# Weight sums of a Strassen pair made together in two buffers, T4 made with T2, and the first down operands fetched among the up products

## The chip, the cores and the metric

The kernel runs on one core of one Trainium2 chip. The metric is the device time of one execution in microseconds (us), the median of the runs shown. The engines are TensorE (PE in the profile's rows, PEld for its weight loads), VectorE (DVE), ScalarE (ACT), GpSimd (POOL) and SyncE (SP), whose queue issues the DMA transfers. Each engine takes its instructions in the order of its own queue and waits on semaphores for the others.

## What is computed

Two transformer blocks in a row, 1024 tokens of width 1024, in f32. Only the two feed-forward networks matter here. In the reference they are

```python
# first block
h = rmsnorm(x, g_ffn[i])
x = x + jnp.square(jax.nn.relu(h @ w_ffn_up[i])) @ w_ffn_down[i]      # 1024 -> 4096 -> 1024
# second block
h = rms_norm(x, g_ffn[l])
up = depthwise_conv(h @ w_up[l], conv_f_w[l], conv_f_b[l], FFN_CONV // 2)   # 1024 -> 2 x 2816, 3 taps
act = jax.nn.gelu(up[..., :D_FF_2], approximate=True) * up[..., D_FF_2:]
x = x + act @ w_down[l]
```

## The kernel before

Every f32 operand is split into a high part rounded to fp32r (`hi`, a copy by ScalarE) and the rest (`lo`, a subtraction by VectorE); a product is three matmuls, high by high, high by low, low by high (`mm3`, L87 to L91). Weights go from DRAM into one of three raw buffers (`wraw`, 128 x 1024, 512 KB) and from there into one of four pairs of split buffers (`whi`, `wlo`).

The **up products** of both networks are made by `strassen` (L1130) with seven products instead of eight (the form of Strassen and Winograd). The contraction of 1024 is halved, and so are the tokens: the normalised input gives the blocks 11, 21 (tokens 0 to 511) and 12, 22 (tokens 512 to 1023), and from these come T1, T2, T3 and T4. Two blocks of 128 weight columns make a pair `j`: the first block holds a11 and a12, the second a21 and a22. From them GpSimd makes the sums S1 = a21 + a22, S2 = S1 - a11 (L1161, L1162), S3 = a11 - a21, S4 = a12 - S2 (L1166, L1167). All four use one buffer `s` with two halves: S1, S2 lie in it until their split is done, then S3, S4 are written over them (S4 reads S2 in its place).

`prep(j, i)` makes the split weights of step `i`: 0 is the raw first block, 1 the sums S1, S2, 2 the sums S3, S4, 3 the block a22. `consume(j, i)` makes the products of the step and adds the results: step 0 the products with 11 and 21, step 1 with T2 and T1, step 2 with T3 and 22, step 3 with T4. One product is 12 matmuls of 128 x 512 into one of six PSUM buffers `p`; VectorE or ScalarE empties it, and GpSimd adds `r` and the "22" result (L1200, L1201, seen in the rows under L1180). `make` finishes a row of results: in the first network the squared relu (L1328), in the second the convolution (ScalarE L1710, VectorE L1711 and L1712), the gelu and the product of both halves (L1728), after which a DMA stores a row of `hid_d`. There are 16 pairs in the first network and 22 in the second. In the loop (L1265 to L1279) the loads of a step are issued three steps ahead (`loads`), `prep` two steps ahead.

**The start.** The last 512 tokens are normalised and transposed in four units (`t_unit`, L1077: two token groups by two halves of the contraction), which give 22, T1, T2, T3; `tf3` and the two `tf` buffers hold what lies between. Meanwhile the step 0 products of the first `npre` pairs run (3 in the first network, 2 in the second). T4 = 21 - T2 is made after that in four units (`t_last`, L1113), two on VectorE and two on GpSimd, spread over the first steps of the loop.

**The turn.** After all up products, `ffn` (L1281) opens the PSUM tiles of the down products (three of 128 x 1024), loads the first down weights, fetches the first rows of `hid_d` (4 rows of 128 in the first network, 2 in the second) into the buffers `hraw`, splits them (`hh`, `hl`), and reads the residual `x` back from DRAM (`xres`, eight tiles of 512 KB); it lies where the buffers of `strassen` lay.

**The order of the queues** is not the order of the code. A planner walks the instructions with a model of their times and puts on each engine's queue the earliest written instruction that is ready in the model; a later one goes ahead where the earlier are not. A buffer is given out again when its last user is done.

Of the kernel before, what the change touches and what calls it, by code (L numbers as in the profile page):

```python
# [27 lines left out]
class Kern:  # L28
# [1048 lines left out]
    def t_unit(self, hs, t0, k0):  # L1077
# [33 lines left out]
        sub(nc.vector, o["T2"][1], f1, f(o["T2"][0]))  # L1111

    def t_last(self, t0, k0):  # L1113

        nc, B = self.nc, self.B
        t = slice((t0 % 4) * P, (t0 % 4 + 2) * P)
        d = (slice(None), slice(k0, k0 + 2), t)
        t2, t4, b21 = ([x[d] for x in B[n]] for n in ("T2", "T4", "21"))
        f = lambda x: x.bitcast(F32)
        a = self.tf3[:, k0 * 256:k0 * 256 + HALF].rearrange("p (k t) -> p k t", k=2)  # L1120
# [9 lines left out]
    def strassen(self, st, w, pairs, sp, make, npre=3):  # L1130
# [21 lines left out]
        def prep(j, i):  # L1152
            tt = nc.gpsimd.tensor_tensor
            if i == 0:
                split(j, 0, raws[j, 0])
                return
            a11, a12 = (raws[j, 0][:, c:c + HALF] for c in (0, HALF))
            a21, a22 = (raws[j, 1][:, c:c + HALF] for c in (0, HALF))
            if i == 1:
                s = ws["s"] = self.sx.tile([P, WCH], F32, tag="s", name="s", bufs=1)  # L1160
                tt(out=s[:, :HALF], in0=a21, in1=a22, op=ALU.add)  # L1161
                tt(out=s[:, HALF:], in0=s[:, :HALF], in1=a11, op=ALU.subtract)  # L1162
                split(j, 1, s)
            elif i == 2:
                s = ws["s"]
                tt(out=s[:, :HALF], in0=a11, in1=a21, op=ALU.subtract)  # L1166
                tt(out=s[:, HALF:], in0=a12, in1=s[:, HALF:], op=ALU.subtract)  # L1167
                split(j, 2, s)
            else:
                split(j, 3, a22)  # L1170
# [38 lines left out]
        seq = [(j, 0) for j in range(npre)]  # L1209
        seq += [(j, i) for j in range(n) for i in range(4) if i or j >= npre]  # L1210
        items = [s for s in seq if s[1] < 3]

        def loads(q):
            if q < len(items):
                j, i = items[q]
                if i == 0 or i == 1 and j < npre:
                    load(j, 0)
                if i == 1:
                    load(j, 1)

# [4 lines left out]
        for q in range(npre):  # L1225
            loads(q)
            prep(*items[q])
            if q == 0:
                for i in range(6):
                    spill(i)  # L1230
# [10 lines left out]
        self.tf3 = self.gp.tile([P, S], F32, tag="gain1024", name="tf3", bufs=self.gb)  # L1241
        hs = self.norm_rows(src, D, gain, (4, 5))
        self.t_unit(hs, 4, 0)
        consume(*seq[0])
# [3 lines left out]
        B["T4"] = [self.sx.tile([P, 4, HALF], F32R, name="T4" + c) for c in "hl"]  # L1248
        self.t_unit(hs, 4, 2)
        consume(*seq[1])  # L1250
        self.t_unit(hs2, 6, 0)
        loads(npre)
        prep(*items[npre])
        self.t_unit(hs2, 6, 2)
        for q in range(2, npre):
            consume(*seq[q])
        rest = [self.t_last(t0, k0) for t0 in (4, 6) for k0 in (0, 2)]
        for r in (rest[0], rest[1], rest[0], rest[2]):
            next(r)
        loads(npre + 1)  # L1260
        prep(*items[npre + 1])
        loads(npre + 2)
        next(rest[2])
        q = npre
        for j, i in seq[npre:]:  # L1265
            if i < 3:
                loads(q + 3)
                if q + 2 < len(items):
                    prep(*items[q + 2])
                q += 1  # L1270
            if i == 2:
                prep(j, 3)
            consume(j, i)
            if rest and j == 0:
                next(rest[1 if i == 1 else 3])
                if i == 1:
                    next(rest[3])
                else:
                    rest = None  # L1279

    def ffn(self, st, nf, w_up, pairs, make, w_down, last=2, gain=None, npre=3):  # L1281
# [3 lines left out]
        self.xs_d = self.dr.tile([S, D], F32, name="xs_d")  # L1285
        with ExitStack() as su:
            self.pp = self.pool(su, "psU", space=PSUM)
            sp = self.pool(su, "sp")
            self.strassen(su, w_up, pairs, sp, make, npre)
# [3 lines left out]
        hid = {}  # L1293

        def fetch(f):
            raw = self.tmp4.tile([P, S], F32, tag="t4", name="hraw")
            nc.sync.dma_start(out=raw, in_=self.hid_d[f * P:(f + 1) * P, :])
            hid[f] = [dp.tile([P, S], F32R, tag="h" + c, name="h" + c, bufs=5) for c in "hl"]
            self.split(*hid[f], raw)
# [3 lines left out]
        for f in range(n):  # L1303
            fetch(f)
# [507 lines left out]
```

## Time and profile before

| | |
|---|---|
| median of 3 runs | 3478.67 us (3476.00 to 3480.02) |
| profiled execution | 3482.99 us, of which span 3481.3 us |
| granted TensorE clock, mean | 0.984 |
| busy: TensorE, VectorE, ScalarE, GpSimd | 3297.0, 1896.1, 1272.3, 599.4 us |
| up products of the first network | about 1135 to 1462 us of the span |
| up products of the second network | about 2725 to 3216 us |

Times in rows count from the span's start. A row of the timeline has start, duration, engine, line, operation, output <- inputs, and in brackets the idle time of the engine before it and who ended it. `SPq` is SyncE's queue. Matmuls are pipelined: one takes 0.39 us from its first to its last word but the next starts after 0.23 us.

### The profile page before, as it was taken

Reading aid. Unit: us, or ns where it says so; the run is one execution under the profiler, and the core shown is the slowest. Engines: PE = TensorE matmul, PEld = TensorE weight load, DVE = VectorE, ACT = ScalarE, POOL = GpSimd, SP = SyncE. Lnnn points to the kernel's source line nnn. Section 1 sums busy time; section 2 is a strip of 40 time slices with the busy share of each in tenths; the row PEclk is TensorE's granted clock in tenths of the full one; section 3 lists DMA queues with packets and bytes.
Section 4 is the critical chain, followed back from the end, with each engine's and each line's share of the span. In section 5 each row is a group of like instructions: output and inputs, shape, how many; then the busy total and the mean of one; then the engine's idle time right before and its main releaser. Section 6 shows DMA issues by size and latency. Waiting matters only on the chain.

```text
span 3481.3 us, 46328 instructions
## 1 busy us (share of the span) xinstructions
PE 3297.0 (95%) x18534; PEld 2696.5 (77%) x18534; DVE 1896.1 (54%) x2829; ACT 1272.3 (37%) x1776; POOL 599.4 (17%) x700
## 2 busy tenths in 40 slices
PE   8999999999989799999999999999999799999899
PEld 8867777777778588788889877777889676776787
DVE  4445666466554654544443466666242866666544
ACT  4342434477422322211122567743121433333211
POOL 0201111122100534200002411100000433333000
PEclk9999999999999899999999999999999999999999
DMA  3532232332372333432221222223353122222521
GB/s 118 169 107 71 74 76 63 92 85 70 123 266 91 106 112 107 167 129 93 90 74 39 96 64 67 66 77 114 123 195 116 65 85 71 71 71 90 184 91 63
DMA packets 362374, 350.89 MB, mean 101 GB/s; under 512 B 88766, under 2 KB 286766, under 8 KB 362158
## 3 DMA queue, kind: packets, MB, share of 16 engines
q1 hardware_dynamic: 362158, 347.93, 31.5%
q8 instruction: 145, 2.38, 0.3%
q14 instruction: 71, 0.58, 0.1%
HBM read 249.29 MB, written 98.58 MB: 100 GB/s over the span
## 4 chain that ended last, share of the span: by engine, by line
PE 61%; DVE 14%; POOL 8%; ACT 6%; issue 6%; DMA 5%; SPq 0%; POOLq 0%; DVEq 0%; ACTq 0%
PE mm L89 16%; PE mm L90 16%; PE mm L91 16%; DVE wlo L59 3%; DMA wraw<-in_w_up_dram 2%; DMA wraw<-in_w_ffn_up_dram 1%; POOL s L1166 1%; POOL s L1167 1%; POOL r L1180 1%; PE p L89 1%; POOL s L1161 1%; PE rps L803 1%; PE p L90 1%; PE p L91 1%; DVE cv L1711 1%
## 5 line engine op out<-in xcount | busy, mean ns | idle before, releaser
L58 ACT CAST whi<-wraw 128x1024 fp32r<-128x1024 f32 (+3 forms) x234 | 232.3, 1001 | 796.9 <-PE mm L91 456.3
L59 DVE TENSOR_TENSOR wlo<-wraw,whi 128x1024 fp32r<-128x1024 f32 (+3 forms) x234 | 279.7, 1203 | 260.7 <-ACT whi L58 255.7
L89 PE MATMUL mm<-whi,hh 128*128 128x512 f32 x864 | 338.1, 393 | 17.2 <-ACT hh L58 12.1
L90 PE MATMUL mm<-wlo,hh 128*128 128x512 f32 x864 | 338.0, 391 | 0.0
L91 PE MATMUL mm<-whi,hl 128*128 128x512 f32 x864 | 336.6, 391 | 0.4 <-DVE hl L59 0.4
L1052 DVE TENSOR_TENSOR xres<-mm,xres 128x512 f32<-128x512 f32 (+1 forms) x272 | 166.4, 653 | 306.4 <-PE mm L91 305.1
L194 POOL TENSOR_SCALAR nst<-nst 128x2 f32<-128x2 f32 (+1 forms) x41 | 9.6, 235 | 1267.5 <-ACT hn L211 1009.2
L89 PEld LDWEIGHTS mm<-whi,hh 128*128 128x128 f32 x864 | 162.8, 189 | 55.4 <-ACT hh L58 12.5
L58 ACT CAST whi<-s 128x1024 fp32r<-128x1024 f32 x76 | 79.9, 1051 | 313.9 <-POOL s L1167 249.8
L91 PEld LDWEIGHTS mm<-whi,hl 128*128 128x128 f32 x864 | 162.8, 189 | 35.6 <-DVE hl L59 1.6
L90 PEld LDWEIGHTS mm<-wlo,hh 128*128 128x128 f32 x864 | 163.3, 189 | 33.8
L89 PE MATMUL mm<-h0h,whi 128*128 128x512 f32 x432 | 167.9, 392 | 3.8 <-ACT h0h L58 1.4
L91 PE MATMUL mm<-h0h,wlo 128*128 128x512 f32 x432 | 169.1, 391 | 0.0
L90 PE MATMUL mm<-h0l,whi 128*128 128x512 f32 x432 | 168.8, 391 | 0.1
L59 DVE TENSOR_TENSOR wlo<-s,whi 128x1024 fp32r<-128x1024 f32 x76 | 97.0, 1276 | 104.9 <-ACT whi L58 104.9
L91 PE MATMUL mm<-h1h,wlo 128*128 128x512 f32 x336 | 131.0, 390 | 0.0
L90 PE MATMUL mm<-h1l,whi 128*128 128x512 f32 x336 | 131.0, 390 | 0.0
L89 PE MATMUL mm<-h1h,whi 128*128 128x512 f32 x336 | 130.7, 390 | 0.0
L89 PE MATMUL p<-h1h,whi 128*128 128x512 f32 x304 | 121.0, 398 | 6.0 <-DVE u L1180 6.0
L89 PE MATMUL p<-h0h,whi 128*128 128x512 f32 x304 | 119.1, 392 | 1.5 <-DVE xres L1052 1.5
L90 PE MATMUL p<-h1l,whi 128*128 128x512 f32 x304 | 119.3, 392 | 0.0
L91 PE MATMUL p<-h0h,wlo 128*128 128x512 f32 x304 | 119.0, 392 | 0.0
(546 smaller groups left out, 8815.4 us busy)
## 6 DMA issues: line engine op xcount, KB each, us to landing
wraw<-in_w_in_dram SPq DMA_DIRECT2D x66, 512.0 KB
hraw<-hid_d SPq DMA_DIRECT2D x54, 512.0 KB
wraw<-in_w_up_dram SPq DMA_DIRECT2D x46, 512.0 KB
wraw<-in_w_ffn_up_dram SPq DMA_DIRECT2D x35, 512.0 KB
hid_d<-o SPq DMA_DIRECT2D x64, 256.0 KB
wraw<-in_w_ffn_down_dram SPq DMA_DIRECT2D x32, 512.0 KB
g<-gate_d SPq DMA_DIRECT2D x24, 512.0 KB
hid_d<-cv SPq DMA_DIRECT2D x22, 512.0 KB
```

Source lines behind the costliest of these rows:

```text
L58: return (self.nc.scalar.copy(out=hi, in_=src), self.nc.vector.tensor_tensor(out=lo, in0=src, in1=hi.bitcast(F32), op=ALU.subtract))
L59: self.nc.vector.tensor_tensor(out=lo, in0=src, in1=hi.bitcast(F32), op=ALU.subtract))
L89: mm(ps, lhsT=sh, rhs=mh, start=first, stop=False)
L90: mm(ps, lhsT=sh, rhs=ml, start=False, stop=False)
L91: mm(ps, lhsT=sl, rhs=mh, start=False, stop=last)
L803: mm(q4(ps)[:, i], lhsT=lhs[:, 4 * h + i], rhs=rhs[:, i], start=True, stop=True)
L1052: self.nc.vector.tensor_tensor(out=o, in0=ps[:, i], in1=o, op=ALU.add)
L1161: tt(out=s[:, :HALF], in0=a21, in1=a22, op=ALU.add)
L1166: tt(out=s[:, :HALF], in0=a11, in1=a21, op=ALU.subtract)
L1167: tt(out=s[:, HALF:], in0=a12, in1=s[:, HALF:], op=ALU.subtract)
L1180: return lambda out: e.tensor_tensor(out=out, in0=a, in1=b, op=ALU.add)
L1711: stt(out=c[:, 1:], in0=u[:, :S - 1], scalar=one("cw0"), in1=c[:, 1:], op0=ALU.mult, op1=ALU.add)
```

## The change

Four things are done. S1, S2 get a buffer `ss[1]` and S3, S4 another, `ss[2]`, which is `tf3`; the four sums of a pair are written one behind the other, in the pair before. The loop over pairs is written out anew with other places for loads, splits and sums. Three of the four T4 units become part of `t_unit` (they use f1 = T2, which is there), on GpSimd; the first is still made by `t_last`, on VectorE. And the first rows of `hid_d` and the first half of the down weights are fetched by `before_last`, called in the last pair between step 1 and step 2, through the `wraw` buffers and into the place of the operands 11 and 21.

```diff
-    def t_unit(self, hs, t0, k0):
+    def t_unit(self, hs, t0, k0, last=True):
...
         sub(nc.vector, o["T2"][1], f1, f(o["T2"][0]))
+        if last:
+            h, l = (f(x[d]) for x in B["21"])
+            sub(nc.gpsimd, f1, h, f1)
+            nc.gpsimd.tensor_tensor(out=f1, in0=f1, in1=l, op=ALU.add)
+            self.t_split(f1, d)
+
+    def t_split(self, src, d):
+        nc, (h, l) = self.nc, (x[d] for x in self.B["T4"])
+        nc.scalar.copy(out=h, in_=src)
+        nc.gpsimd.tensor_tensor(out=l, in0=src, in1=h.bitcast(F32), op=ALU.subtract)
 
     def t_last(self, t0, k0):
...
-        tt = (nc.gpsimd if k0 else nc.vector).tensor_tensor
-        tt(out=a, in0=f(b21[0]), in1=f(t2[0]), op=ALU.subtract)
-        tt(out=a, in0=a, in1=f(t2[1]), op=ALU.subtract)
-        tt(out=a, in0=a, in1=f(b21[1]), op=ALU.add)
-        yield
-        nc.scalar.copy(out=t4[0], in_=a)
-        tt(out=t4[1], in0=a, in1=f(t4[0]), op=ALU.subtract)
-        yield
+        a = self.tmp4.tile([P, S], F32, tag="t4", name="t4f")[:, :HALF].rearrange("p (k t) -> p k t", k=2)
+        tt = self.nc.vector.tensor_tensor
+        f = lambda n, c: self.B[n][c][d].bitcast(F32)
+        tt(out=a, in0=f("21", 0), in1=f("T2", 0), op=ALU.subtract)
+        tt(out=a, in0=a, in1=f("T2", 1), op=ALU.subtract)
+        tt(out=a, in0=a, in1=f("21", 1), op=ALU.add)
+        self.t_split(a, d)
...
         def prep(j, i):
+            split(j, i, raws[j, 0] if i == 0 else raws[j, 1][:, HALF:] if i == 3 else ss[i])
+
+        def sums(j, i):
...
+            s1, s2, s3, s4 = (ss[q][:, c:c + HALF] for q in (1, 2) for c in (0, HALF))
             if i == 1:
-                s = ws["s"] = self.sx.tile([P, WCH], F32, tag="s", name="s", bufs=1)
...
+                tt(out=s1, in0=a21, in1=a22, op=ALU.add)
+                tt(out=s2, in0=s1, in1=a11, op=ALU.subtract)
             else:
-                split(j, 3, a22)
+                tt(out=s4, in0=a12, in1=s2, op=ALU.subtract)
+                tt(out=s3, in0=a11, in1=a21, op=ALU.subtract)
...
+        self.tf3 = ss[2] = self.gp.tile([P, S], F32, tag="gain1024", name="tf3", bufs=self.gb)
         hs = self.norm_rows(src, D, gain, (4, 5))
+        self.t_unit(hs, 4, 0, False)
+        consume(0, 0)
         hs2 = self.norm_rows(src, D, gain, (6, 7))
...
+        ss[1] = self.sx.tile([P, WCH], F32, name="s12")
         self.t_unit(hs, 4, 2)
+        sums(0, 1)
+        consume(1, 0)
         self.t_unit(hs2, 6, 0)
+        prep(0, 1)
         self.t_unit(hs2, 6, 2)
+        sums(0, 2)
+        load(1, 0)
+        self.t_last(4, 0)
+        for j in range(2, npre):
+            consume(j, 0)
+        for j in range(n):
+            if j >= npre:
+                consume(j, 0)
+            prep(j, 3)
+            prep(j, 2)
+            if j + 1 < n:
+                load(j + 1, 1)
+            consume(j, 1)
+            if j + 1 < n:
+                if j + 1 >= npre:
+                    prep(j + 1, 0)
+            else:
+                before_last()
+            if j + 2 < n:
+                load(j + 2, 0)
+            consume(j, 2)
+            if j + 1 < n:
+                sums(j + 1, 1)
+                sums(j + 1, 2)
+            consume(j, 3)
+            if j + 1 < n:
+                prep(j + 1, 1)
...
+        def fetch(f, raw, place):
+            nc.sync.dma_start(out=raw, in_=self.hid_d[f * P:(f + 1) * P, :])
+            hid[f] = place
+            self.split(*hid[f], raw)
+
+        def before_last():
+
+            n = nf % 4 or 4
+            place = [t.rearrange("p k t -> p (k t)").rearrange("p (k t) -> p k t", k=4) for t in self.first()]
+            for f in range(n):
+                fetch(f, self.wps[0].tile([P, WCH], F32, tag="wraw", name="hraw", bufs=self.wrb),
+                      [t[:, f] for t in place])
+            pre.extend(self.load_chunks(w_down, 0, n, cols[:1]))
...
-        pre = self.load_chunks(w_down, 0, n, cols)
-        for f in range(n):
-            fetch(f)
+        pre.extend(self.load_chunks(w_down, 0, len(hid), cols[1:]))
```

The later rows of `hid_d` are fetched as before, through `tmp4`.

## Rows read from the trace of the kernel before

**Rows 1.** Busy us of each engine in six stretches; the first line names the columns.
```profile
core 0: us, PE busy (x) PEld busy (x) DVE busy (x) ACT busy (x) POOL busy (x), PEclk, DMA share, GB/s
...
1179.60:1187.30 7.70, 5.61 (x12) 3.97 (x13) 4.44 (x4) 1.68 (x2) 4.54 (x4) 0.50 0.42 138
1188.00:1462.00 274.00, 273.90 (x1209) 226.33 (x1208) 141.56 (x186) 68.05 (x88) 104.17 (x82) 1.00 0.38 122
2745.80:2788.70 42.90, 32.77 (x120) 25.43 (x121) 38.51 (x31) 15.45 (x19) 32.05 (x19) 0.86 0.09 25
2790.00:3216.00 426.00, 396.14 (x1674) 308.52 (x1673) 270.82 (x278) 158.95 (x181) 147.99 (x116) 1.00 0.24 76
3216.60:3228.80 12.20, 0.18 (x1) 0.00 (x0) 10.49 (x11) 4.53 (x4) 2.48 (x2) 0.71 0.81 271
3228.80:3235.30 6.50, 6.09 (x14) 4.34 (x15) 3.58 (x3) 1.04 (x1) 0.00 (x0) 0.50 0.95 322
```

**Rows 2.** Waits of TensorE, 2600 to 3240 us: total us, times, longest.
```profile
PE p L89 <- DVE u L1180: 27.5, 33, 1.7
PE mm L89 <- ACT hh L58: 12.1, 1, 12.1
```

**Rows 3.** Chain of waits through one pair of the second network: start, us, what.
```profile
3153.79 1.23 DVE wlo L59
3155.15 1.29 POOL s L1166
3156.44 1.26 POOL s L1167
3157.72 3.80 DMA wraw<-in_w_up_dram
3161.66 1.28 POOL s L1161
3163.02 1.29 POOL s L1162
3164.31 1.25 POOL r L1180
```

**Rows 4.** Waits of GpSimd and VectorE, 2790 to 3216 us.
```profile
POOL s L1166 <- DVE wlo L59: 190.7, 19, 10.2
POOL s L1161 <- DMA wraw<-in_w_up_dram: 73.6, 19, 4.5
...
DVE u L1180 <- POOL r L1180: 93.0, 20, 5.4
```

**Rows 5.** VectorE's timeline, second network: a convolution's two steps, an add between.
```profile
3145.96 1.27 DVE L1711 SCALAR_TENSOR_TENSOR cv<-u,vcol_conv_f_b,cv 128x1023 f32<-128x1023 f32 x1
3147.15 0.68 DVE L1180 TENSOR_TENSOR u<-p,tf 128x512 f32<-128x512 f32 x1
3147.75 1.27 DVE L1712 SCALAR_TENSOR_TENSOR cv<-u,vcol_cw,cv 128x1023 f32<-128x1023 f32 x1
```

**Rows 6.** Waits of TensorE, 1100 to 1500 us.
```profile
PE p L89 <- ACT T4h L1126: 13.2, 1, 13.2
...
PE mm L89 <- DVE o L1180: 3.5, 1, 3.5
```

**Rows 7.** Timelines of VectorE, TensorE and GpSimd in the first network's start.
```profile
1140.28 0.68 DVE L1097 TENSOR_TENSOR T2l<-tf,T2h 128x512 fp32r<-128x512 f32 x1
...
1149.70 0.67 PE L89 MATMUL p<-T2h,whi 128*128 128x512 f32 x1 [1.19 <-ACT T2h L1110]
...
1156.78 2.14 POOL L1124 TENSOR_TENSOR tf<-tf,h0l 128x512 f32<-128x512 f32 x1
```

**Rows 8.** VectorE's timeline, "12" adds of the second network's last two pairs.
```profile
3205.66 0.69 DVE L1180 TENSOR_TENSOR u<-p,r 128x512 f32<-128x512 f32 x1 [1.47 <-POOL r L1180]
...
3220.73 0.69 DVE L1180 TENSOR_TENSOR u<-p,r 128x512 f32<-128x512 f32 x1 [1.46 <-POOL r L1180]
```

**Rows 9.** VectorE's and GpSimd's timelines, second network, two steps that overlap.
```profile
2774.58 1.86 POOL L1161 TENSOR_TENSOR s<-wraw 128x512 f32<-128x512 f32 x1 [1.49 <-DMA wraw<-in_w_up_dram]
...
2775.23 2.30 DVE L1711 SCALAR_TENSOR_TENSOR cv<-u,vcol_conv_f_b,cv 128x1023 f32<-128x1023 f32 x1
```

**Rows 10.** VectorE's groups by form, 2790 to 3216 us: busy us, mean ns, idle before.
```profile
L1180 DVE TENSOR_TENSOR u<-p,r 128x512 f32<-128x512 f32 x40 | 27.5, 688 | 93.0 <-POOL r L1180 93.0
```

More of the change, by code (lines that the diff above doesn't have):

```diff
@@ L1111, in t_unit, with strassen @@
         sub(nc.vector, o["T2"][1], f1, f(o["T2"][0]))
+        if last:
[7 more added lines that the diff above has]
+        nc.gpsimd.tensor_tensor(out=l, in0=src, in1=h.bitcast(F32), op=ALU.subtract)
     def t_last(self, t0, k0):
[L1115 removed]
         t = slice((t0 % 4) * P, (t0 % 4 + 2) * P)
         d = (slice(None), slice(k0, k0 + 2), t)
[L1118 to L1130 removed]
+        a = self.tmp4.tile([P, S], F32, tag="t4", name="t4f")[:, :HALF].rearrange("p (k t) -> p k t", k=2)
[5 more added lines that the diff above has]
+        self.t_split(a, d)
+    def strassen(self, st, w, pairs, sp, make, npre, before_last):
         nc = self.nc
@@ L1152, in prep @@
         def prep(j, i):
+            split(j, i, raws[j, 0] if i == 0 else raws[j, 1][:, HALF:] if i == 3 else ss[i])
+        def sums(j, i):
             tt = nc.gpsimd.tensor_tensor
-            if i == 0:
-                split(j, 0, raws[j, 0])
-                return
             a11, a12 = (raws[j, 0][:, c:c + HALF] for c in (0, HALF))
             a21, a22 = (raws[j, 1][:, c:c + HALF] for c in (0, HALF))
+            s1, s2, s3, s4 = (ss[q][:, c:c + HALF] for q in (1, 2) for c in (0, HALF))
             if i == 1:
-                s = ws["s"] = self.sx.tile([P, WCH], F32, tag="s", name="s", bufs=1)
[L1161 to L1168, printed above, removed]
-            else:
-                split(j, 3, a22)
+                tt(out=s1, in0=a21, in1=a22, op=ALU.add)
+                tt(out=s2, in0=s1, in1=a11, op=ALU.subtract)
+            else:
+                tt(out=s4, in0=a12, in1=s2, op=ALU.subtract)
+                tt(out=s3, in0=a11, in1=a21, op=ALU.subtract)
+        ss = {}
         def product(j, i, q, b):
@@ L1208, in strassen @@
         n = len(pairs)
[L1209 to L1219, printed above, removed]
         self.sx = None
@@ L1224, in strassen @@
         spill = lambda i: nc.sync.dma_start(out=x_d[i * P:(i + 1) * P, :], in_=x[i])
[L1225 to L1230, printed above, removed]
+        for j in range(npre):
+            load(j, 0)
+            prep(j, 0)
+        for i in range(6):
+            spill(i)
+        load(0, 0)
+        load(0, 1)
         for i in (6, 7):
@@ L1248, in strassen @@
         B["T4"] = [self.sx.tile([P, 4, HALF], F32R, name="T4" + c) for c in "hl"]
+        ss[1] = self.sx.tile([P, WCH], F32, name="s12")
         self.t_unit(hs, 4, 2)
-        consume(*seq[1])
+        sums(0, 1)
+        consume(1, 0)
         self.t_unit(hs2, 6, 0)
-        loads(npre)
-        prep(*items[npre])
+        prep(0, 1)
         self.t_unit(hs2, 6, 2)
[L1255 to L1279, printed above, removed]
+        sums(0, 2)
[25 more added lines that the diff above has]
+                prep(j + 1, 1)
     def ffn(self, st, nf, w_up, pairs, make, w_down, last=2, gain=None, npre=3):
@@ L1285, in ffn @@
         self.xs_d = self.dr.tile([S, D], F32, name="xs_d")
+        hid, pre = {}, []
+        cols = [(0, 512), (512, 512)]
+        def fetch(f, raw, place):
[9 more added lines that the diff above has]
+            pre.extend(self.load_chunks(w_down, 0, n, cols[:1]))
         with ExitStack() as su:
@@ L1288, in ffn @@
             sp = self.pool(su, "sp")
-            self.strassen(su, w_up, pairs, sp, make, npre)
+            self.strassen(su, w_up, pairs, sp, make, npre, before_last)
         self.pp = self.pool(st, "psD", space=PSUM)
@@ L1292, in ffn @@
         dp = self.pool(st, "hid")
[L1293 to L1299, printed above, removed]
-        cols = [(0, 512), (512, 512)]
-        n = nf % 4 or 4
-        pre = self.load_chunks(w_down, 0, n, cols)
-        for f in range(n):
-            fetch(f)
+        pre.extend(self.load_chunks(w_down, 0, len(hid), cols[1:]))
         xp = self.pool(self.xst, "x", side="right")
@@ L1311, in ffn @@
             n = (nf - f0) % 4 or 4
-            for f in range(max(f0 + 1, len(hid)), min(f0 + n + 1, nf)):
-                fetch(f)
+            for f in range(len(hid), min(f0 + n + 1, nf)):
+                fetch(f, self.tmp4.tile([P, S], F32, tag="t4", name="hraw"),
+                      [dp.tile([P, S], F32R, tag="h" + c, name="h" + c, bufs=5) for c in "hl"])
             x = lambda k, hf: [t[:, hf * HALF:(hf + 1) * HALF] for t in hid[f0 + k]]
```

3 lines of the change are left out of this document (removed).

## The prediction

> **What bounds the kernel now.** I first read the busy time by stretches [rows 1], because the change touches only the two feed-forward networks and their ends. In the up products of the first network TensorE is busy for all of 274.0 us with 1209 matmuls, 0.2266 us each; a pair of column blocks is 7 products of 12 matmuls, so 84 x 0.2266 = 19.04 us is the pace that TensorE can hold. In the second network the like stretch has 1674 matmuls (19.93 pairs) in 426.0 us, 21.38 us a pair: 1674 x 0.2266 = 379.4 us, so 46.6 us are lost, though both stretches run at the full granted clock, 2.4 GHz. Around them stand shorter losses: the starts, and the turn from up to down products.
>
> Next the waits of TensorE [rows 2]: in the second network it waits 33 times for VectorE's adds (L1180), which free a product's PSUM buffer, and once 12.1 us for the first down operand. So VectorE is late, although it is busy for only 270.8 of 426 us. The chain of waits says why [rows 3]: the low split of S1, S2 releases GpSimd's S3 (1.29 us), S4 (1.26 us) frees a raw weight buffer, the load of the next pair's second weight block takes 3.80 us, S1 and S2 of the next pair follow, and only behind them does GpSimd reach the add r of this pair, for which VectorE holds the evacuation of the "22" product. The list of waits puts sizes on it [rows 4]: over 19 pairs S3 waits 190.7 us for the split, S1 73.6 us for the load, and the add 93.0 us (20 pairs, 4.65 us each) for r. This loop, not an engine's work, makes 21.4 us a pair. In the first network VectorE has no convolution to do and the same loop fits under 19.04 us.
>
> Queues are not in written order [rows 5]: the "21" add is written behind both steps of a convolution and runs between them. The planner fills a gap with later work that is ready.
>
> In the first network's start TensorE waits 13.2 us for T4 and at the turn 3.5 us for VectorE [rows 6]; T4's last part starts only when GpSimd gets to it (its steps there take up to 2.14 us [rows 7]), and behind the wait TensorE ran at half clock, 1.2 GHz, for 7.7 us [rows 1].
>
> **The change, part by part.** Durations are those of the one profiled execution, 3482.99 us (span 3481.3 us, 1.7 us around it). It stands 4.3 us above the median of 3478.67, so I subtract from 3482.99 and then take 4.3 off.
>
> *Sums in two buffers, up loop (second network).* Compute is the same: four sums, four splits, two loads a pair. What goes is the tie: S3, S4 no longer wait for the split of S1, S2, and all four are written ahead of the pair's last product. Moved past on GpSimd: sums now stand behind r and the "22" sum of the pair before, not ahead of them. On SP the two loads stand a half pair earlier in the written loop; a load waits for S4 of an earlier pair, and behind it in SP's queue wait a pair's stores, which nobody needs for a long time. The splits move too: that of S1, S2 is written behind the whole evacuation of a pair, 24 matmuls (5.4 us) ahead of its use; hidden only if the planner pulls it forward, as it does now [rows 5]. What is late next? Either TensorE (19.04) or VectorE beside GpSimd. VectorE alone: from the "12" add of the last pair but one to that of the last, where no sums stand on GpSimd, it took 3220.73 - 3205.66 = 15.07 us [rows 8]. The sums come back beside its work: a convolution step that meets one took 2.30 instead of 1.27 us [rows 5, 9], 1.03 us more. Four of them: 15.07 + 4 x 1.03 = 19.2 us. Bounds: 19.04 (nothing collides) and 21.0, VectorE and GpSimd strictly one after the other (270.8 + 148.0 us over 19.93 pairs [rows 1]). The 15.07 + 4.1 is the nearest; with 0.2 us for hand-overs I take **19.4**. That gives back 0.36 x 19.93 = 7.2 of 46.6 us: a gain of **39.4** us, ends 46.6 and 7.
>
> The Trainium skill, SBUF — State Buffer, section Who interferes with whom, speaks against putting GpSimd's sums beside VectorE: a VectorE instruction with two SBUF inputs and a GpSimd instruction that reads SBUF shut each other out, and the one issued second waits for the end of the first. The trace agrees (1.27 against 2.30 us). It leaves adds that read PSUM free, five of 0.69 us a pair [rows 10]: 21.0 - 3.4 = 17.6 us of exclusive time, so by the rule alone the period would be TensorE's 19.04 and this term 46.6.
>
> In the first network the loop is already at TensorE's pace; no gain, and no loss as long as VectorE (141.6 of 274 us) keeps its room.
>
> *T4 beside T2, start of the first network.* Before, two of four T4 units were VectorE's and two GpSimd's, 4 steps each; now three are GpSimd's altogether, the fourth only in its last step: GpSimd 10 steps for 8, VectorE 3 for 8, ScalarE 4 as before. The new cost is order: S3, S4 of pair 0 go into the buffer that the units use for T3 (L1095), so they stand behind the last T3 unit and, on GpSimd, behind T4. From the second unit's T2 (1140.28 + 0.68 [rows 7]) GpSimd has 14 steps up to S3, about 1.5 us each (1.29 to 2.14 [rows 3, 7]): 1141 + 21 = 1162; split 1163. TensorE starts T2 at 1149.7 [rows 7], has 36 matmuls (8.2 us) besides T3, waits some 4 us, then does T3, T4 with half of it at half clock: 1171. The next pair's S1 waits for a raw buffer that S4 frees: 1162 + 3.8 + 2.6 + a split of 1 = 1169.5, in time. TensorE got there at 1187.3 before, with about 1 us of the next product done: gain 15, I take **14**. Ends: 24 (60 matmuls from 1149.7 without a wait end at 1163.3) and 4 (GpSimd at 2.14 us a step: split at 1172, then 24 matmuls at half clock, 0.46 us each as in the 6.5 us stretch [rows 1], end at 1183).
>
> *The same start, second network.* 42.9 us for 120 matmuls, which need 27.2 [rows 1]: 15.7 lost. TensorE has one product pair less to hide GpSimd's steps (two blocks are prepared, not three). Lost in my count above: 1171 - 1149.7 - 13.6 = 8; some 3.5 more here: gain **4**, ends 12 and -5.
>
> *First down operands in the last pair.* Two fetches (four in the first network) and one (two) weight loads are issued on SP through the three raw weight buffers, their splits into the buffer of operands 11 and 21, free after the last pair's first two products, 60 matmuls (13.6 us) before the turn. Behind the splits' wait on ScalarE stand copies of the last pair; the planner places a split when its load can have landed. VectorE has room, since no next pair's splits come. In the second network TensorE stood 12.2 us, then 14 matmuls took 6.5 us at half clock for 3.2 [rows 1]: 15.5 in all. What stays is the evacuation of the last product, some 3.5 us as in the first network [rows 6]. The x reload, 4.19 MB at the 322 GB/s seen there, 13 us, is now met sooner; three PSUM tiles of 2.7 us cover 8 of it: 1 us more. Gain **11**, ends 15 and 2. In the first network the turn is 3.5 us, bound by VectorE: gain **1.5**, ends 3.5 and -2. The second half of the down weights is loaded after the turn's start in the written order; it is needed 5.4 us or more later and its buffers free during the last pair: nothing, at worst the 3.8 us of a load.
>
> Sum: 39.4 + 14 + 4 + 11 + 1.5 = 69.9. 3482.99 - 69.9 = 3413.1, less 4.3: **3408.8**, say 3409.
>
> **Rivals.** (a) *VectorE and GpSimd become the bound*: the sums hit more often, six steps instead of four, and in-order queues leave gaps; 20.5 us a pair, near the serial 21.0. For it: 2.30 against 1.27. Against: five adds read PSUM, and TensorE may run six PSUM buffers ahead. The loop then gains 46.6 - 1.46 x 19.93 = 17.5: 3431. The skill's rule above is the reason; taken alone it does not reach 20.5.
>
> (b) *GpSimd's backlog eats the starts*: 2.14 us a step instead of 1.5 puts S3 9 us later; the starts give 2 instead of 18: 3425.
>
> (c) *The loop stays*: the load still lands too late, behind SP's queue, and a pair takes 21.38: only 30.5 of gain: 3448. Against: S4 no longer waits for a split.
>
> (d) *Slower: the written order becomes the queue's.* Then the split of S1, S2 is VectorE's last work of a pair, and TensorE stops at T2 of every pair of the second network: the rest of T2 and T1, 22 matmuls, 5.0 us, then VectorE's chain of 15.07 with four collisions, 4.1: 24.2 us a pair, 2.8 x 19.93 = 56 lost, less the 30.5 won elsewhere: 3504. It decides above 21.38 + 30.5 / 19.93 = 22.9 us a pair. Against it: [rows 5], and operands that today are split well before use.
>
> **Numbers.** Forecast 0.62 (its own range 3388 to 3428), (a) 0.16, (b) 0.10, (c) 0.05, (d) 0.07. The range 3386 to 3446 takes in the forecast, (b), nearly all of (a). No change means within 0.2%, about 7 us, which is what a measurement of this kernel can tell: only the tails between (c) and (d), 0.03. Slower 0.07, faster 0.90.
>
> **What would show it.** Right: 1674 matmuls of the second network's up products in 379 to 390 us; r no longer behind S1, S2; the wait for T4 gone, a smaller one for T3 in its place; no wait for hh at the turn. Wrong: VectorE's two-input steps at 2.3 us throughout (a); TensorE waiting for the low split at T2 in each pair (d); starts that last as long as now (b).

## The result and the profile after

The changed kernel takes **3416.36 us** in the median of 4 runs (3413.16 to 3416.72) beside 3477.34 for the kernel before in the same series: a ratio of 0.9823, 95% interval 0.9806 to 0.9840. The forecast was 3409, range 3386 to 3446. The profiled execution is 3416.02 us (span 3414.3), 67.0 us shorter than the one before.

To see where these went I cut both spans at the same matmuls: a network's first up product, the last T4 matmul of pair 1, the last up product, the first down product. Times in us:

| stage | before | after | gain | forecast |
|---|---|---|---|---|
| up to the first up product (same program) | 1123.9 | 1117.0 | 6.9 | 0 |
| first network, start, through pair 1's T4 | 76.9 | 64.3 | 12.6 | 14 |
| first network, loop | 261.6 | 267.7 | -6.1 | 0 |
| first network, turn | 3.9 | 4.5 | -0.6 | 1.5 |
| second network, start, through pair 1's T4 | 67.7 | 67.2 | 0.5 | 4 |
| second network, loop | 427.8 | 382.3 | 45.5 | 39.4 |
| second network, turn | 12.5 | 5.9 | 6.6 | 11 |
| down products and all between | 1507.0 | 1505.4 | 1.6 | 0 |

The first row is no effect of the change: it is the same program, and the kernels of the experiments took 1114.0 to 1123.6 us there. Without it some 60 us are left, of which the second loop is three quarters.

Busy time by stretches, after (columns as in rows 1): first network's start and loop, then the second's start, loop and turn.

```profile
1117.00:1181.30 64.30, 53.01 (x215) 42.05 (x216) 51.10 (x55) 23.04 (x38) 44.40 (x30) 0.89 0.28 89
1181.30:1449.00 267.70, 263.03 (x1153) 217.10 (x1152) 142.99 (x185) 70.70 (x87) 108.64 (x82) 0.99 0.41 129
...
2708.30:2775.40 67.10, 49.84 (x194) 39.16 (x192) 47.99 (x52) 27.62 (x43) 45.55 (x30) 0.82 0.20 62
2776.00:3157.50 381.50, 380.65 (x1679) 314.59 (x1678) 291.77 (x286) 160.89 (x185) 166.03 (x117) 1.00 0.28 89
3157.70:3163.60 5.90, 0.42 (x3) 0.05 (x1) 5.63 (x6) 2.59 (x4) 2.86 (x2) 0.71 0.64 206
```

The line from 2776 us on answers [rows 1]: where 1674 matmuls took 426.0 us, 1679 take 381.5, and TensorE is busy for 380.65 of them: 0.227 us a matmul, 19.1 us a pair. The loop runs at TensorE's pace.

The waits of TensorE, second network (2700 to 3200 us), which answer [rows 2]:

```profile
PE tr L1087 <- DVE tf L1097: 11.7, 3, 6.2
PE mm L89 <- DVE u L1181: 5.5, 1, 5.5
PE p L89 <- ACT whi L58: 3.1, 1, 3.1
```

Of the 33 waits for VectorE's adds one of 0.7 us is left, and the wait for `hh` is gone; the turn now waits 5.5 us for VectorE's last add. The rest lies in the start. The first network (1100 to 1480 us, [rows 6]):

```profile
PE p L89 <- ACT whi L58: 5.7, 1, 5.7
...
PE p L89 <- DVE o L1181: 2.4, 1, 2.4
PE p L91 <- DVE a22l L59: 2.3, 1, 2.3
```

The 13.2 us for T4 became 5.7 us for the split of pair 0's S3, S4, ahead of T3. The other two lines, at pair 2's T4, are new.

The waits of GpSimd and VectorE in the second loop (2776 to 3157 us), which answer [rows 4]:

```profile
POOL s L1166 <- DVE wlo L59: 179.4, 18, 10.1
...
DVE u L1181 <- POOL r L1181: 85.2, 20, 4.5
```

GpSimd's wait for the load is gone. But its wait for the low split is as long as ever: it has moved from S3 to S1. And VectorE still waits 4.3 us a pair for r. One pair in the timelines of GpSimd and then VectorE (L1166, L1167 are S1, S2; L1169 S4, L1170 S3) shows the way round, to be laid beside [rows 3] and [rows 8]:

```profile
3060.43 1.30 POOL L1166 TENSOR_TENSOR s<-wraw 128x512 f32<-128x512 f32 x1 [10.13 <-DVE wlo L59]
3061.81 2.16 POOL L1167 TENSOR_TENSOR s<-s,wraw 128x512 f32<-128x512 f32 x1
3064.05 1.29 POOL L1169 TENSOR_TENSOR tf<-wraw,s 128x512 f32<-128x512 f32 x1
3065.30 1.30 POOL L1170 TENSOR_TENSOR tf<-wraw 128x512 f32<-128x512 f32 x1
3066.55 1.29 POOL L1181 TENSOR_TENSOR r<-r,tf 128x512 f32<-128x512 f32 x1
```

```profile
3049.08 0.69 DVE L1181 TENSOR_TENSOR u<-p,r 128x512 f32<-128x512 f32 x1 [4.43 <-POOL r L1181]
...
3059.13 1.22 DVE L59 TENSOR_TENSOR wlo<-s,whi 128x1024 fp32r<-128x1024 f32 x1
...
3060.87 1.94 DVE L59 TENSOR_TENSOR wlo<-tf,whi 128x1024 fp32r<-128x1024 f32 x1
3062.74 0.68 DVE L1181 TENSOR_TENSOR tf<-p,r 128x512 f32<-128x512 f32 x1
3067.87 0.69 DVE L1181 TENSOR_TENSOR u<-p,r 128x512 f32<-128x512 f32 x1 [4.46 <-POOL r L1181]
```

The low split of S1, S2 (3059.13) frees their buffer, S1 of the next pair goes into it at once, the four sums follow, **r only behind them**, then VectorE's "12" add (3067.87), and from there its evacuation down to the next low split. So the loop of before is still closed (a chain of waits that comes back to its own first step, one pair later, and so has a period of its own), but shorter, since the load is no longer in it: from one "12" add to the next 18.79 us. Its margin to TensorE's 19.04 is 0.25 us. Before, two "12" adds lay 21.82 us apart:

```profile
3143.76 0.69 DVE L1180 TENSOR_TENSOR u<-p,r 128x512 f32<-128x512 f32 x1 [4.93 <-POOL r L1180]
...
3165.58 0.69 DVE L1180 TENSOR_TENSOR u<-p,r 128x512 f32<-128x512 f32 x1 [4.95 <-POOL r L1180]
```

### The profile page after: what moved, and what is told of

Its sections match the earlier page's. It is cut to its first block, busy times and chain, and to the rows that moved or that the text cites. A ratio compares the mean times of both kernels' runs of the same rounds, so it can differ in the third digit from the quotient of the medians.

```text
span 3414.3 us, 46299 instructions
## 1 busy us (share of the span) xinstructions
PE 3277.0 (96%) x18534; PEld 2701.3 (79%) x18534; DVE 1898.1 (56%) x2819; ACT 1273.8 (37%) x1776; POOL 628.2 (18%) x704
## 4 chain that ended last, share of the span: by engine, by line
PE 76%; DVE 9%; ACT 5%; issue 4%; POOL 3%; DMA 2%; SPq 0%; DVEq 0%; ACTq 0%; POOLq 0%
PE mm L89 16%; PE mm L90 16%; PE mm L91 16%; PE p L91 6%; PE p L89 6%; PE p L90 6%; PE rps L803 1%; PE tr L236 1%; PE lr L89 1%; PE tp L507 1%; PE rps L719 1%; DVE wlo L59 1%; PE lr L90 1%; DVE sq L1529 1%; PE lr L91 1%
## 5 line engine op out<-in xcount | busy, mean ns | idle before, releaser
L59 DVE TENSOR_TENSOR wlo<-wraw,whi 128x1024 fp32r<-128x1024 f32 (+3 forms) x234 | 281.0, 1209 | 266.9 <-ACT whi L58 261.3
L89 PE MATMUL mm<-whi,hh 128*128 128x512 f32 x768 | 298.4, 391 | 1.4 <-ACT whi L58 1.4
L90 PE MATMUL mm<-wlo,hh 128*128 128x512 f32 x768 | 298.9, 389 | 0.0
L91 PE MATMUL mm<-whi,hl 128*128 128x512 f32 x768 | 298.6, 389 | 0.0
L89 PEld LDWEIGHTS mm<-whi,hh 128*128 128x128 f32 x768 | 143.5, 188 | 34.3 <-ACT whi L58 4.8
L91 PEld LDWEIGHTS mm<-whi,hl 128*128 128x128 f32 x768 | 144.1, 188 | 30.2 <-DVE hl L59 0.2
L90 PEld LDWEIGHTS mm<-wlo,hh 128*128 128x128 f32 x768 | 144.2, 188 | 30.0
L1709 ACT ACTIVATE cv<-u,vcol_conv_f_b,vcol_cw 128x1024 f32<-128x1024 f32 x44 | 54.8, 1246 | 207.7 <-DVE u L1181 136.3
L90 PE MATMUL p<-h0l,whi 128*128 128x512 f32 x304 | 119.9, 394 | 0.0
```

What stands on the lines that cost most here:

```text
L59: self.nc.vector.tensor_tensor(out=lo, in0=src, in1=hi.bitcast(F32), op=ALU.subtract))
L89: mm(ps, lhsT=sh, rhs=mh, start=first, stop=False)
L90: mm(ps, lhsT=sh, rhs=ml, start=False, stop=False)
L91: mm(ps, lhsT=sl, rhs=mh, start=False, stop=last)
L1709: nc.scalar.activation(out=c, in_=u, func=AF.Identity, scale=one("cw1"), bias=one("conv_f_b"))
```

## The experiments

My theory after the comparison: the shared buffer made the second loop, and all of it; what is left is a loop of 18.79 us. Rivals: the order, the loads, or collisions between VectorE and GpSimd.

**Two buffers alone.** Into the kernel before, S3, S4 in `tf3`:

```diff
-                s = ws["s"]
+                s2 = ws["s"]
+                s = self.tf3 if j else s2
...
-                tt(out=s[:, HALF:], in0=a12, in1=s[:, HALF:], op=ALU.subtract)
+                tt(out=s[:, HALF:], in0=a12, in1=s2[:, HALF:], op=ALU.subtract)
```

> The kernel before with one edit: S3, S4 of every pair but the first go into tf3 and not over S1, S2; loads, splits, T4 and the turn stay where they were. Theory (the shared buffer made the loop): from the end of pair 1's T4 product to the last product of the second network 382 to 390 us where before has 427.9 and after 382.3; time about 3434 us, nearly all of the loop's gain. Rival 1 (the new places of loads, sums and splits made it): 420 to 428 us, time 3470 to 3477. Rival 2 (both are needed): between, about 405 us and 3455.

3418.76 us, ratio 0.9835 (0.9816 to 0.9854); second loop 387.5. In this kernel pair 1's S3, S4 overwrite part of the working of T4, so T4 comes out wrong and the starts are not to be used. With `j > 1` in place of `j` that does not happen:

> The kernel before with e1's edit from pair 2 on only (pairs 0 and 1 keep the one buffer), so that nothing is overwritten while T4 is worked out. Theory: the second buffer acts in the steady loop, so the loop of the second network is 386-391 us as in e1 (387.5) and the time 3417-3424. Rival: e1 was short because part of T4's work was spoiled early; then the start or the loop is longer by more than 4 us.

3425.47 us, ratio 0.9860 (0.9844 to 0.9875). Its starts are 4.4 and 5.1 us longer than in the kernel just shown (75.5 and 72.0 for 71.1 and 66.9), so the rival holds for them: that time was too short. The loop is shorter than expected. The second loop and turn:

```profile
2791.00:3172.70 381.70, 381.70 (x1682) 315.93 (x1680) 291.91 (x283) 161.82 (x181) 161.04 (x117) 1.00 0.27 86
3172.70:3178.30 5.60, 0.39 (x3) 0.01 (x1) 5.38 (x5) 3.29 (x3) 0.00 (x0) 0.72 0.85 304
```

The profile shows no idle time of TensorE in the loop. Some 50 of the 61 us (3475.76 - 3425.47, the kernel before in the same series) come from the second buffer; the loop written out anew has no part in them. And the turn fell from 12.5 to 5.6 us **without the early fetch**. SyncE's timeline of before (below it VectorE's last split ahead of the fetch) and of this kernel says how:

```profile
3216.96 6.43 SPq L78 DMA_DIRECT2D wraw<-in_w_down_dram  x3
3223.50 0.41 SPq L1297 DMA_DIRECT2D hraw<-hid_d  x1
```

```profile
3221.34 1.66 DVE L59 TENSOR_TENSOR wlo<-wraw,whi 128x1024 fp32r<-128x1024 f32 x1
```

```profile
3167.07 5.81 SPq L78 DMA_DIRECT2D wraw<-in_w_down_dram  x2
3172.99 0.41 SPq L1298 DMA_DIRECT2D hraw<-hid_d  x1
```

The fetch stands in SyncE's queue behind loads of down weights, and those wait for raw buffers that VectorE's low splits free (the last in the kernel before ended at 3223.00, in this one at 3172.49). In the kernel before VectorE was late, and the fetch went out 7.1 us after the last product had started (3216.4); here 0.3 us after it (3172.7).

**The early fetch taken back**, after the change (`before_last` out, the rows fetched behind the loop as before):

```diff
-            else:
-                before_last()
...
```

> The changed kernel without the early fetch: first rows and first down weights are asked for after the up products, through tmp4, as before. Theory (the early fetch gives the second network's turn and nothing in the first): last up product to first down matmul 12 us in the second network (before 12.4, after 5.9), 3.5 to 5 in the first (before 3.9, after 4.6); time 3423 to 3427. Rival (with VectorE no longer late the late fetch is hidden too): 6 us, time 3416 to 3418.

3412.05 us (3411.07 to 3413.18), ratio 0.9817 (0.9802 to 0.9831); turns 2.3 and 5.7 us. The rival holds: in the changed kernel the early fetch brings nothing that can be told. In the first network it costs 2.2 us at the turn, as one more split stands ahead of VectorE's last add; in the second the wait for `hh` is back and VectorE's is gone, of nearly the same length (5.3 us for 5.5). That is not so in every kernel: where VectorE is earlier at the end of the second loop, the early fetch gives a turn of 2.9 to 3.1 us (four of the kernels below), and the one below that fetches late has 5.7.

**T4 late**, after the change: all four units behind T2, two on VectorE and two on GpSimd.

```diff
-        if last:
+        if False:
...
-        tt = self.nc.vector.tensor_tensor
+        tt = (self.nc.gpsimd if k0 else self.nc.vector).tensor_tensor
...
-        self.t_last(4, 0)
+        for t0 in (4, 6):
+            for k0 in (0, 2):
+                self.t_last(t0, k0)
```

> The changed kernel with T4 made as before: all four units after T2 is whole, two on VectorE and two on GpSimd. Theory (T4 beside T2 is what shortens the first network's start): from the first up product to the end of pair 1's T4 product 74 to 78 us in the first network (before 76.9, after 64.3), 70 to 75 in the second (before 67.7, after 67.1); time 3428 to 3436. Rival (the start is shorter because sums and loads come earlier): 64 to 67 us in the first network, time 3416 to 3420.

3423.16 us (3417.17 to 3426.17), ratio 0.9849 (0.9827 to 0.9870), between theory and rival. Start and loop together: first network 71.5 + 263.5 = 335.0 us for 332.0, second 71.8 + 380.8 = 452.6 for 449.4. So T4 beside T2 is worth some 3 us in each network, and in the first the start's gain of 7.2 is given back by 4.2 in the loop.

**S1 made twice**, to lengthen the remaining loop by a known amount:

```diff
                 tt(out=s1, in0=a21, in1=a22, op=ALU.add)
+                tt(out=s1, in0=a21, in1=a22, op=ALU.add)
```

> The changed kernel with S1 made twice for every pair: one more GpSimd step of some 1.3 us, same result. Theory (the loop split of S1, S2 -> four sums -> r -> 12 add -> VectorE's chain -> next split is still closed; it now takes 18.79 us, 0.25 under TensorE's 19.04): 1.0 to 1.3 us more in the loop, 19.8 to 20.1 a pair, the second network's loop 16 to 21 us longer (398 to 403 us), time 3432 to 3438; the first network unchanged. Rival (TensorE is the bound with room to spare, VectorE idle 4.4 us a pair): loop 382 to 384 us, time 3416 to 3419.

3448.68 us (3446.80 to 3451.08), ratio 0.9922 (0.9907 to 0.9937); loop 404.5, somewhat above what was expected. The first network, expected unchanged, takes 3.9 us more in start and loop and 1.6 at the turn, the second turn 4.8 more. Two "12" adds on VectorE:

```profile
2993.95 0.69 DVE L1182 TENSOR_TENSOR u<-p,r 128x512 f32<-128x512 f32 x1 [5.82 <-POOL r L1182]
...
3014.10 0.69 DVE L1182 TENSOR_TENSOR u<-p,r 128x512 f32<-128x512 f32 x1 [5.82 <-POOL r L1182]
```

20.15 us: the 18.79 of the changed kernel plus 1.36, where one sum takes 1.29. GpSimd still stands idle for 10 us in each pair, and yet the instruction costs its length less the margin: (1.36 - 0.25) x 20 pairs = 22.2, and the loop grew by 404.5 - 382.3 = 22.2. The loop is closed, and its margin is the one that was read off.

**The same with a second buffer for S1, S2**, the pairs taking turns, which opens that loop:

```diff
+            if i == 1:
+                ss[1] = s12[j % 2]
...
-        ss[1] = self.sx.tile([P, WCH], F32, name="s12")
+        s12 = [self.sx.tile([P, WCH], F32, name="s12"),
+               self.gp.tile([P, S], F32, tag="gain1024", name="s12b", bufs=self.gb)]
```

> The kernel after, with the first sum of each pair made twice as in e4, and a second buffer for the first two sums, the pairs taking turns. Theory: what set e4's period (20.2 us a pair) is the loop sum -> low split on VectorE -> sum of the next pair into the same buffer; with a second buffer the loop is open, GpSimd has about 10.5 us of work in a period of 19.04, and the loop of the second network falls back from 404.5 us to 381-385, the time to 3412-3419. Rival: GpSimd's and VectorE's work, longer where they collide, is itself the bound; then the loop stays at 398 or more and the time above 3435.

3438.47 us (3436.56 to 3444.52), ratio 0.9899 (0.9885 to 0.9912); loop 395.9. Neither is right: 8.6 of the 22.2 us are back, the rest not. GpSimd's wait for the low split has turned into one for the load, as its timeline and then VectorE's say:

```profile
3004.14 1.49 POOL L1168 TENSOR_TENSOR s<-wraw 128x512 f32<-128x512 f32 x1 [8.57 <-DMA wraw<-in_w_up_dram]
...
3012.66 1.29 POOL L1184 TENSOR_TENSOR r<-r,tf 128x512 f32<-128x512 f32 x1
```

```profile
2994.35 0.69 DVE L1184 TENSOR_TENSOR u<-p,r 128x512 f32<-128x512 f32 x1 [4.45 <-POOL r L1184]
...
2999.56 0.68 DVE L59 TENSOR_TENSOR a22l<-wraw,a22h 128x512 fp32r<-128x512 f32 x1
```

Behind the first loop lies a second: "12" add (2994.35), low split of a22, which frees a raw buffer (3000.24), load (3.8 us from its issue at 3000.27, landed 3004.08), five sums and r (3013.95), next "12" add: 2994.35 to 3013.98, 19.6 us. It is the loop of [rows 3] with another split in it. The rival has a part in its length: two of the five sums and a low split meet, and take 2.1 to 2.3 us instead of 1.2 to 1.3; but VectorE is not full, since it waits 87.4 us for r in this stretch.

**The second buffer alone**, after the change:

> The kernel after with a second buffer for the first two sums and nothing else. Theory: TensorE's pace (19.04 us a pair) bounds the loop already, so the loop of the second network stays at 380.5-382; VectorE, whose turn of 18.79 us had 0.25 us to spare, now runs ahead, so its last add comes earlier and the second turn falls from 5.9 to 3-4.5 us; time 3412-3416. Rival: the loop of the sums still costs TensorE single waits (11.7 us on VectorE's turns of T, 5.5 on its additions); then the loop falls below 378 and the time below 3411.

3411.48 us (3410.11 to 3413.91), ratio 0.9819 (0.9805 to 0.9832). As the theory had it: loop 380.8, TensorE busy for all of it, second turn 3.1. The start is longer by 2.2, for TensorE waits 4.5 us for the split ahead of T3 and 2.5 for T4's low part, where it was 3.1 and 1.3; start and loop are 450.2 for 449.4. The second buffer does not set VectorE free: its "12" adds lie 18.55 to 18.59 us apart, and GpSimd's S1 now waits 8.4 us a pair for the load. The next chain is only 0.2 us shorter than the one that was opened.

**Sums behind r**, after the change, the order that the prediction stated:

```diff
-            if j + 1 < n:
-                sums(j + 1, 1)
-                sums(j + 1, 2)
             consume(j, 3)
             if j + 1 < n:
+                sums(j + 1, 1)
+                sums(j + 1, 2)
                 prep(j + 1, 1)
```

> The kernel after with all four sums of the next pair written behind the present pair's last product, in both networks, so that GpSimd makes r and u first. It is the order that the prediction took the change to have. Theory: the sums have about 8 us to spare before ScalarE splits them, so the loop of the second network stays at 380.5-382.5, VectorE is released by r earlier and its turn no longer touches 19.04, the second turn falls to 3-4.5, and the first network's loop loses its stall at pair 2's T4 (267.7 to 261-264): time 3406-3412. Rival: r waits for VectorE's addition of T3's product, the sums start behind it, 3 to 5 us later than now, and TensorE waits for their split: loop of the second network 395 or more, time above 3425.

3413.11 us (3410.12 to 3413.60), ratio 0.9819 (0.9806 to 0.9833); loops 266.2 and 382.0, turns 4.5 and 5.9, all as after the change. Neither theory was tested, for GpSimd's queue came out the same:

```profile
3001.56 1.29 POOL L1166 TENSOR_TENSOR s<-wraw 128x512 f32<-128x512 f32 x1 [10.13 <-DVE wlo L59]
...
3006.41 1.30 POOL L1170 TENSOR_TENSOR tf<-wraw 128x512 f32<-128x512 f32 x1
3007.66 1.29 POOL L1181 TENSOR_TENSOR r<-r,tf 128x512 f32<-128x512 f32 x1
```

The planner puts the sums ahead of r in both places where they were written. What r ahead of the sums would give stays open.

**The first network's start.** Pair 0's S3, S4 in a tile of their own instead of `tf3`:

```diff
+        ss[2] = self.tmp4.tile([P, S], F32, tag="t4", name="s34")
         sums(0, 2)
...
             prep(j, 2)
+            ss[2] = self.tf3
```

> The kernel after, with the last two sums of pair 0 alone put into a spare working tile and not into tf3, where T3 is still worked out at that time. Theory: TensorE's wait of 5.7 us ahead of pair 0's T3 in the first network comes from the fourth sum waiting for the last unit of T3 to leave tf3; it goes, the first network's start falls from 64.3 us to 58-60, the second's by 0 to 3, and the time to 3407-3412. Rival: the sums are late because GpSimd is still at its parts of T2 and T4; then the starts stay within 1 us of 64.3 and 67.2 and the time stays at 3416.

3413.23 us (3411.41 to 3419.19), ratio 0.9827 (0.9814 to 0.9840). The wait of 5.7 us went, and the start became 66.4 us, not shorter: TensorE now waits 4.6 us for T2. Pair 0's S4 is made early, in its own tile; but now pair 1's S3, S4 go into `tf3`, and its S4 stands on GpSimd behind the last unit of T3 (done at 1151.83). On ScalarE the planner has the split of these sums ahead of a copy that makes T2, and it waits there for S4. The tie to `tf3` has moved from pair 0 to pair 1. TensorE's timeline, GpSimd's (S4 of pair 0 and of pair 1) and ScalarE's:

```profile
1156.82 0.80 PE L89 MATMUL p<-T2h,whi 128*128 128x512 f32 x1 [4.59 <-ACT T2h L1110]
```

```profile
1125.58 1.28 POOL L1169 TENSOR_TENSOR s<-wraw,s 128x512 f32<-128x512 f32 x1 [2.79 <-PE tr L1087]
...
1153.46 1.70 POOL L1169 TENSOR_TENSOR tf<-wraw,s 128x512 f32<-128x512 f32 x1
```

```profile
1155.20 1.04 ACT L58 CAST whi<-tf 128x1024 fp32r<-128x1024 f32 x1 [4.42 <-POOL tf L1169]
1156.15 0.61 ACT L1110 CAST T2h<-tf 128x512 fp32r<-128x512 f32 x1
```

Start and loop are 332.0 us, as after the change. Late fetch, own tile and second buffer together did no better:

> Three edits together on the kernel after: the down operands fetched after the loop as before the change, the last two sums of pair 0 in a tile of their own, and a second buffer for the first two sums. If they add up: 4 us from the fetch, 4 to 8 from the tile, 0 to 3 from the buffer, time 3400-3408. If they take the same time from one wait, it stays at e3's 3412, give or take 2.

3421.54 us (3414.85 to 3422.89), ratio 0.9843 (0.9830 to 0.9857): slower than either expectation: the first start is 71.0 us, 338.4 with the loop. The edits do not add up; what makes that start longer still was not followed further.

**The stall at pair 2's T4**, which ate half of the start's gain. GpSimd's timeline after the change (S4 of pair 2, then S1, S3 of pair 3, r), and VectorE's:

```profile
1176.91 1.62 POOL L1169 TENSOR_TENSOR tf<-wraw,s 128x512 f32<-128x512 f32 x1
1185.87 1.29 POOL L1166 TENSOR_TENSOR s<-wraw 128x512 f32<-128x512 f32 x1 [7.34 <-DVE wlo L59]
...
1190.98 1.30 POOL L1181 TENSOR_TENSOR r<-r,tf 128x512 f32<-128x512 f32 x1
```

```profile
1184.57 1.23 DVE L59 TENSOR_TENSOR wlo<-wraw,whi 128x1024 fp32r<-128x1024 f32 x1 [3.22 <-ACT whi L58]
1185.71 0.68 DVE L1181 TENSOR_TENSOR tf<-p,r 128x512 f32<-128x512 f32 x1
1193.54 0.69 DVE L1327 SCALAR_TENSOR_TENSOR o<-o 128x512 f32<-128x512 f32 x1 [7.14 <-POOL o L1181]
```

S4 of pair 2 frees a raw buffer at 1178.53; pair 3's first load goes out then and lands at 1183.4, its second, 1.1 us behind it, at 1185.7, just before S1 starts (the profile names a split that ended at the same time). Pair 3's split stands ahead of pair 1's T3 add on VectorE, its sums ahead of pair 1's r on GpSimd. VectorE idles 7.14 us, PSUM buffers stay full, and TensorE stops twice, 2.4 and 2.3 us. From 1196 to 1201 us its granted clock is 0.66, between its two levels, 2.4 and 1.2 GHz. In a kernel with the second buffer and the fetch late in the first network alone, the sums of pair 3 were written later:

```diff
-            if j + 1 < n:
+            if j + 1 < n and (j != 2 or npre == 2):
                 sums(j + 1, 1)
                 sums(j + 1, 2)
             consume(j, 3)
+            if j == 2 and npre > 2:
+                sums(3, 1)
+                sums(3, 2)
```

> The kernel after with three edits where the traces left time: the second buffer for the first two sums (e7), the four sums of pair 3 of the first network written behind pair 2's last product, and the down operands of the first network fetched after its loop, those of the second before the end of it. Theory: the first network's loop (267.9 us in e7) holds one stall of 6 us, at pair 2's T4, because GpSimd has the sums of pair 3, whose load is late, ahead of pair 2's r; it goes, loop 261-263; its turn falls from 4.5 to 2.3; the second network keeps e7's 380.8 and 3.1. Time 3402-3406. Rival: the stall only moves, to the products of pair 3 that now wait for their sums; then the loop stays at 266 or more and the time at 3408-3412.

3409.93 us (3407.02 to 3412.03), ratio 0.9812 (0.9798 to 0.9825). The turns are 2.3 and 3.0, as expected, but the stall stays (TensorE waits 0.6 and 2.3 us there, loop 266.9): again GpSimd's order there did not change, so the move of the sums was not tested. And r that waits is pair 1's, not pair 2's as I wrote. So in this kernel, with the sums written as after the change, the two adds of pair 1 went to VectorE:

```diff
+                g = V if j == 1 and npre > 2 else G
-                add(G, u2, r5[j])(u2)
-                make(j, "22", add(G, u3, r5.pop(j)))
+                add(g, u2, r5[j])(u2)
+                make(j, "22", add(g, u3, r5.pop(j)))
```

> The kernel of e9 with the written order of the sums as after the change, and with the two additions of pair 1 that GpSimd makes in the first network (r and the 22 result) put on VectorE. Theory: the stall of 6 us at pair 2's T4 comes from GpSimd's queue, where these two stand behind all four sums of pair 3, which wait for a late load; VectorE, idle from its T3 addition on, makes them at once, the PSUM buffer comes free before TensorE needs it, and the first network's loop falls from 266.9 to 261-263.5 us, the time to 3403-3407. Rival: VectorE and ScalarE are late themselves, because the split of the same load stands ahead of the T3 addition in their queues; then the loop stays at 265 or more and the time at 3409-3411.

3412.19 us (3410.79 to 3422.73), ratio 0.9828 (0.9814 to 0.9841). The stall at pair 2's T4 is gone, as the theory said; it comes back at pair 3's T3, where the same thing happens one pair later (TensorE, GpSimd):

```profile
1209.96 0.80 PE L89 MATMUL p<-T3h,whi 128*128 128x512 f32 x1 [5.01 <-DVE o L1183]
```

```profile
1201.01 1.29 POOL L1168 TENSOR_TENSOR s<-wraw 128x512 f32<-128x512 f32 x1 [12.45 <-DMA wraw<-in_w_ffn_up_dram]
...
1206.10 1.26 POOL L1183 TENSOR_TENSOR r<-r,tf 128x512 f32<-128x512 f32 x1
```

Start and loop are 335.2 us for 332.0. So the stall hangs on r behind the sums, whichever pair it is; that the late load holds the sums up is read from the rows and not shown by an edit, since how to bring the loads of pairs 2 to 4 earlier was not tried.

Of all kernels the one with buffer and late first fetch has the lowest median, 0.2% below the changed kernel; the intervals of their ratios overlap, so it is not shown to be faster.

## Why the prediction was right, and where it was not

**The direction, the size and the main cause were right.** The shared buffer made the loop, its size was 46.6 us, and 45.5 came back; the second buffer alone, in the kernel before, shows it. Rivals (a), (b), (c) did not occur: 19.1 us a pair, and starts that gained 13 us together, before the loop's give-back. Rival (d) did not occur either; that the written order does not reach GpSimd's queue two kernels showed.

**The period, 19.4, was mis-sized**: four collisions of 1.03 us were added to VectorE's 15.07. By groups of form in the second loop, the convolution's steps (L1710, L1711) meet no sum; two low splits do (one that meets none takes 1.22 us in the pair shown above):

```profile
L1710 DVE SCALAR_TENSOR_TENSOR cv<-u,vcol_conv_f_b,cv 128x1023 f32<-128x1023 f32 x40 | 52.0, 1299 | 1.4 <-ACT cv L1709 1.4
L59 DVE TENSOR_TENSOR wlo<-tf,whi 128x1024 fp32r<-128x1024 f32 x20 | 37.3, 1866 | 0.0
L59 DVE TENSOR_TENSOR wlo<-wraw,whi 128x1024 fp32r<-128x1024 f32 x21 | 34.6, 1647 | 1.8 <-ACT whi L58 1.8
```

That is 0.65 + 0.43 = 1.1 us a pair in place of 4.1, and the 0.43 stood in the 15.07 already: in that stretch a split of this form took 1.69 us too (at 3206.27). What VectorE's turn has in place of collisions is the wait for r, 4.3 us a pair: 18.79 with it. The sum thus named the wrong second bound, and that 19.4 came near the 19.1 measured is luck. The Trainium skill, SBUF — State Buffer, section Who interferes with whom, left adds that read PSUM free and by itself gave TensorE's pace, 46.6: here it was nearer than my number, and the trace agrees with its detail too. The split issued at 3060.87 ends 1.08 us after the end of S1 (3061.73), S2 ends 1.16 us after the end of that split, while the add from PSUM at 3062.74 takes its 0.68 us beside S2.

**"Sums now stand behind r" was wrong.** They stand ahead of it, so one of the signs named for being right, r no longer behind S1, S2, did not come. I had read in [rows 5] that queues are not in written order, and then took the written order for this step. The tie through S1's buffer, which follows from it, was not in my account; that it did no harm is a matter of 0.25 us.

**The first start, 14, was right (12.6); that it is kept was not.** Counted from the first up product, S4 of pair 0 was forecast 38.1 us in (1162) and done 36.2 us in (1153.26), T3 waited 5.7 us where some 4 were said, and pair 0's last T4 matmul started 50.7 us in for 47.1. What I missed is behind the start: r and a load late at pairs 1 to 3, 6.1 us. T4 beside T2 alone is worth 3 us a network.

**The second start, 4, brought 0.5**: TensorE's 11.7 us for VectorE at the transposes and 3.1 for the split stand where the wait for T4 stood. It lies within the bounds given.

**The second turn, 11, was mis-sized and put down to the wrong edit.** 6.6 us came, and the two buffers alone bring as much (6.9): SyncE's queue was late because VectorE was. The 3.5 us for the last product's evacuation became 5.5, because the early splits stand ahead of it on VectorE. They cost that much only because VectorE is late: with the second buffer the same splits stand there, the last "12" add comes 1.2 us ahead of the last product's start instead of 1.7 behind it, and TensorE waits 2.7 us. In the first turn, -0.6 for 1.5, the splits again.

By size: loop +6.1 on my sum, the first network -9.6, second start -3.5, second turn -4.4; together the 11 us between 69.9 and 58.5. That the time came within 7 us of the forecast owes something to luck: the loop's error offsets a third of the others. In the medians 3478.67 - 3416.36 = 62.3, as some of the rest that the change doesn't touch was shorter too.

## What to carry to other kernels

When a wait in a closed chain is cut, write down the next chain that closes over the same instructions and its length beside the bounding engine's pace: here 21.8 us became 18.8, and behind that lay one by way of the load. Before costing an order, find out whether the written order reaches the queue. A queue that is late at the end of a loop can make a turn look like a late fetch: see first whether the loop's own fix takes it away, and cost the early fetch again after it.

## What the runs showed that I had not expected

One more GpSimd instruction of 1.29 us a pair, on an engine that is idle for half of the time, cost the kernel 32 us (3448.68 - 3416.36): 22.2 because it lay in a loop with 0.25 us of margin, the rest in the first network and at the turns. And start and loop of the first network take 331.6 to 332.4 us in the changed kernel and in five others (fetch late, own tile, second buffer, sums behind r, and the one with the lowest median): whichever wait went, another of its length came. What sets that sum was not found.
